# Moving the full loads of a softmax cross entropy from SyncE's ring to GpSimd's software ring

## Chip, cores, metric

The kernel runs on one core of one Trainium2 chip. The metric is the device time of one execution in microseconds (us), the median of the runs; a profiled execution gives the traces. The "span" of a profile is the profiled time of the core's instructions; it is about 2 us shorter than the metric.

Words used here: a *ring* is the queue in which the transfers of one issuing engine (SyncE, GpSimd) wait for the 16 DMA engines; a *descriptor* is one contiguous piece of a transfer; a *packet* is what the profile lists as one record of a DMA engine. A *gather* is a small transfer that fetches 128 single logits from addresses held in a tile. The *flag* is `single_packet=True` on a load.

## The reference

```python
def reference(logits, labels):            # logits [16, 512, 32000] float32, labels [16, 512]
    logits_max = np.max(logits, axis=-1, keepdims=True)
    log_sum_exp = np.log(np.sum(np.exp(logits - logits_max), axis=-1)) + logits_max.squeeze(-1)
    log_probs = logits - log_sum_exp[..., np.newaxis]
    loss = -log_probs[np.arange(batch)[:, None], np.arange(seq), labels]
    return loss.astype(np.float32)
```

1048.6 MB of logits must be read once. The kernel sums exponentials without subtracting the maximum, and fetches the 8192 logits at the labels by gathers.

## The kernel before

The 8192 rows are 128 partitions x 64 groups of 32000 logits. Three buffers of 128 x 16000 float32 (64000 B in each partition) take the loads in turn. Loads are numbered in order: 0, 1, 2 (4000, 4000 and 8000 columns) fill the first buffer, 3 to 126 fill one buffer each, and the last dozen, 127 to 138, are shorter, so that little work is left when the last byte lands.

```python
    plan(0, [[4000, 4000, 8000], [16000]], [(0, 0), (0, 1), (0, 2), (1, 0)])
    for g in range(1, G - 2):
        plan(g, [[W], [W]], [(0, 0), (1, 0)])
    ...                                                    # cut: the short last loads
    data = ctx.enter_context(tc.tile_pool(name="data", bufs=3))
    ...                                                    # cut: small tiles
    nc.scalar.dma_start(out=labs64[:], in_=labels_pg)
    nc.gpsimd.iota(idx[:], pattern=[[V, G]], base=0, channel_multiplier=G * V)
    nc.gpsimd.tensor_tensor(out=idx[:], in0=idx[:], in1=labs32, op=ALU.add)
    for g in range(G):                                     # 64 gathers of 128 single logits
        nc.gpsimd.indirect_dma_start(out=lab_logit[:, g:g + 1], out_offset=None, in_=lg,
            in_offset=bass.IndirectOffsetOnAxis(ap=idx[:, g:g + 1], axis=1))
    ...
    for j, (g, b, at, n) in enumerate(loads):
        ...                                                # cut: a new tile t for each buffer number b
        nc.sync.dma_start(out=t[:, at:at + n], in_=lg_pg[:, g, c0:c0 + n])
        exp(g, t[:, at:at + n])                            # ScalarE, in place, with a row sum
```

A load into a buffer waits until the exponential three buffers back has run.

The softmax here doesn't subtract the row's maximum and nothing guards it: scores larger than these inputs give would overflow.

## Time and profile before

| | before |
|---|---|
| time | 2435.71 us (2435.50 to 2435.98, 3 runs; the result below has a fourth) |
| rate over the span | 431 GB/s |
| ScalarE busy | 72% |
| one full load, mid-run (start of exponential to start of exponential) | 18.90 us, 8.192 MB: 433.5 GB/s |
| its exponential with the accumulator read | 13.64 us, then 5.27 us idle |

From the profile page of the kernel before: busy time of the engines, busy tenths of the DMA engines in 40 slices, and the packets, MB and share of 16 engines of its two main rings (q1 is SyncE's, q0 GpSimd's software ring).

```profile
...
DVE 1.3 (0%) x5; ACT 1748.9 (72%) x281; POOL 61.0 (3%) x70
...
DMA  9999999999999999999999999999999999999998
...
q1 hardware_dynamic: 20304, 1048.62, 99.8%
q0 software_dynamic: 2048, 0.04, 0.1%
...
```

The DMA engines are over 90% busy in every slice but the last, which has 80%: this kernel is bound by the loads. The 20304 packets of SyncE's ring are one for each partition row of each load (8 on each of 16 engines), one semaphore packet per engine and load (4 bytes that report the landing), and the outputs.

From the timeline of ScalarE before (start and duration in us; in brackets the idle time before it and what ended it), at the start, mid-run and at the end:

```profile
...
8.32 3.54 ACT L105 ACTIVATE t<-t 128x4000 f32<-128x4000 f32 x1 [5.86 <-DMA t<-in_logits_dram]
...
13.00 3.54 ACT L105 ACTIVATE t<-t 128x4000 f32<-128x4000 f32 x1 [1.05 <-DMA t<-in_logits_dram]
...
23.02 6.87 ACT L105 ACTIVATE t<-t 128x8000 f32<-128x8000 f32 x1 [6.39 <-DMA t<-in_logits_dram]
...
42.12 13.54 ACT L105 ACTIVATE t<-t 128x16000 f32<-128x16000 f32 x1 [12.13 <-DMA t<-in_logits_dram]
...
61.53 13.54 ACT L105 ACTIVATE t<-t 128x16000 f32<-128x16000 f32 x1 [5.79 <-DMA t<-in_logits_dram]
...
80.69 13.54 ACT L105 ACTIVATE t<-t 128x16000 f32<-128x16000 f32 x1 [5.52 <-DMA t<-in_logits_dram]
...
1597.17 13.54 ACT L105 ACTIVATE t<-t 128x16000 f32<-128x16000 f32 x1 [5.26 <-DMA t<-in_logits_dram]
...
1616.06 13.54 ACT L105 ACTIVATE t<-t 128x16000 f32<-128x16000 f32 x1 [5.27 <-DMA t<-in_logits_dram]
...
2372.73 13.54 ACT L105 ACTIVATE t<-t 128x16000 f32<-128x16000 f32 x1 [5.26 <-DMA t<-in_logits_dram]
...
2400.52 6.37 ACT L105 ACTIVATE t<-t 128x7400 f32<-128x7400 f32 x1 [0.46 <-DMA t<-in_logits_dram]
...
2430.02 1.00 ACT L105 ACTIVATE t<-t 128x960 f32<-128x960 f32 x1
...
```

The first six lines are the exponentials of loads 0 to 5, each run as soon as its load lands. Mid-run, starts lie 18.89 us apart with 5.26 us of idle time: ScalarE always waits for a DMA. The first of the ten short last loads make ScalarE wait 0.3 to 0.5 us each, the later ones 0.1 us or less, and the last exponential starts at 2430.02.

From the windows of the kernel before (the stretch in us, busy time of three engines, the granted clock, the DMA share, GB/s):

```profile
...
40.00:130.00 90.00, 0.00 (x0) 65.30 (x9) 19.72 (x21) 1.00 1.00 423
78.50:84.50 6.00, 0.00 (x0) 3.81 (x1) 1.88 (x2) 1.00 0.99 416
...
```

These stretches are shown for the comparison further down. 423 GB/s is less than 433.5 as gathers run here.

### The profile page before, as it was taken

The numbers are of one execution on the slowest core, as the hardware profiler recorded it, in microseconds if no ns is written. First come the engines' busy times: TensorE is split into PE (matmuls) and PEld (weight loads), VectorE is DVE, ScalarE is ACT, GpSimd is POOL, SyncE is SP. The second block draws the span as 40 slices with busy tenths as digits, with TensorE's granted clock in tenths as the row PEclk, the third lists the DMA queues.
The fourth block names the chain that finished last, engine by engine and source line by source line (L and its number), as shares of the span: only waits on it lengthen the run. The fifth ranks groups of instructions, "written<-read, shape, count | busy, mean of one in ns | idle before, by whom it ended". The sixth has DMA issues, their size and how long they took to land.

```text
span 2434.1 us, 807 instructions
## 1 busy us (share of the span) xinstructions
DVE 1.3 (0%) x5; ACT 1748.9 (72%) x281; POOL 61.0 (3%) x70
## 2 busy tenths in 40 slices
DVE  0000000000000000000000000000000000000000
ACT  4777766777677776777677776777667776777769
POOL 3222000000000000000000000000000000000000
DMA  9999999999999999999999999999999999999998
GB/s 421 422 421 433 425 438 431 427 438 438 433 426 436 438 434 426 435 438 434 426 435 436 435 430 431 436 435 430 431 436 438 431 427 436 438 433 426 438 433 377
DMA packets 22502, 1048.77 MB, mean 431 GB/s; under 512 B 4576, under 2 KB 4704, under 8 KB 5216
## 3 DMA queue, kind: packets, MB, share of 16 engines
q1 hardware_dynamic: 20304, 1048.62, 99.8%
q0 software_dynamic: 2048, 0.04, 0.1%
q10 hardware_dynamic: 144, 0.07, 0.0%
q14 instruction: 6, 0.05, 0.0%
HBM read 1048.67 MB, written 0.03 MB: 431 GB/s over the span
## 4 chain that ended last, share of the span: by engine, by line
DMA 76%; ACT 24%; issue 0%; SPq 0%; ACTq 0%; DVE 0%
DMA t<-in_logits_dram 76%; ACT t L105 24%; SPq L113 0%; ACTq L105 0%; ACT logsum_last L127 0%; DVE res_last L128 0%; ACT logsum L120 0%
## 5 line engine op out<-in xcount | busy, mean ns | idle before, releaser
L105 ACT ACTIVATE t<-t 128x16000 f32<-128x16000 f32 (+5 forms) x139 | 1734.8, 12481 | 681.4 <-DMA t<-in_logits_dram 681.2
L89 POOL DMA_INDIRECT lab_logit<-in_logits_dram,idx x64 | 60.3, 942 | 178.3 <-DMA lab_logit<-in_logits_dram,idx 174.5
L105 ACT ACTIVATION_READ_ACCUMULATOR t<-t 128x1 f32 x139 | 25.9, 186 | 0.0
L84 ACT ACT_TABLE_LOAD x1 | 1.3, 1283 | 1.2 <-PEq L144 1.2
L118 DVE TENSOR_REDUCE totals<-sums 128x63 f32<-128x315 f32 x1 | 0.5, 480 | 2398.9 <-ACT t L105 2398.9
L87 POOL TENSOR_TENSOR idx<-idx,labs 128x64 int32<-128x64 int32 x1 | 0.3, 322 | 7.5 <-DMA labs<-in_labels_dram 7.5
L85 DVE MEMSET sums<- 128x315 f32 x1 | 0.3, 321 | 0.9 <-PEq L144 0.9
L127 ACT ACTIVATE logsum_last<-sums_last,part 128x1 f32<-128x1 f32 x1 | 0.3, 294 | 0.0
L121 DVE TENSOR_TENSOR res<-logsum,lab_logit 128x63 f32<-128x63 f32 x1 | 0.2, 225 | 25.3 <-ACT logsum L120 25.3
L120 ACT ACTIVATE logsum<-totals 128x63 f32<-128x63 f32 x1 | 0.2, 238 | 0.0
L86 POOL IOTA idx<- 128x64 int32 x1 | 0.2, 172 | 0.4 <-PEq L155 0.4
L123 DVE TENSOR_REDUCE part<-sums_last 128x1 f32<-128x9 f32 x1 | 0.2, 163 | 4.0 <-ACT t L105 4.0
L128 DVE TENSOR_TENSOR res_last<-logsum_last,lab_logit 128x1 f32<-128x1 f32 x1 | 0.2, 159 | 1.2 <-ACT logsum_last L127 1.2
L144 POOL MEMSET const-uint8-127<- 128x1 uint8 x1 | 0.1, 118 | 0.0
L144 POOL MEMSET const-bfloat16-1.0<- 128x1 bf16 x1 | 0.1, 113 | 0.0
L144 POOL MEMSET const-float32-0.0<- 128x1 f32 x1 | 0.1, 98 | 0.2 <-issue 0.2
L144 POOL MEMSET const-float32-1.0<- 128x1 f32 x1 | 0.1, 104 | 0.0
## 6 DMA issues: line engine op xcount, KB each, us to landing
t<-in_logits_dram SPq DMA_DIRECT2D x124, 8000.0 KB, 43.0
t<-in_logits_dram SPq DMA_DIRECT2D x1, 5000.0 KB, 35.9
t<-in_logits_dram SPq DMA_DIRECT2D x2, 2000.0 KB, 9.6
t<-in_logits_dram SPq DMA_DIRECT2D x1, 4000.0 KB, 21.4
t<-in_logits_dram SPq DMA_DIRECT2D x1, 3700.0 KB, 32.9
t<-in_logits_dram SPq DMA_DIRECT2D x1, 3000.0 KB, 42.6
t<-in_logits_dram SPq DMA_DIRECT2D x1, 2920.0 KB, 39.5
t<-in_logits_dram SPq DMA_DIRECT2D x1, 2270.0 KB, 26.4
```

The costliest lines, as they stand in the source:

```text
L84: nc.scalar.preload_act_table_set("natural_log_exp_and_others")
L85: nc.vector.memset(sums[:], 0.0)
L86: nc.gpsimd.iota(idx[:], pattern=[[V, G]], base=0, channel_multiplier=G * V)
L87: nc.gpsimd.tensor_tensor(out=idx[:], in0=idx[:], in1=labs32, op=ALU.add)
L89: nc.gpsimd.indirect_dma_start(out=lab_logit[:, g:g + 1], out_offset=None, in_=lg, in_offset=bass.IndirectOffsetOnAxis(ap=idx[:, g:g + 1], ...
L105: nc.scalar.activation(out=ap, in_=ap, func=EXP, accum_out=s)
L118: nc.vector.reduce_sum(out=totals[:], in_=sums[:], axis=X)
L120: nc.scalar.activation(out=logsum[:], in_=totals[:], func=LN)
L121: nc.vector.tensor_tensor(out=res[:], in0=logsum[:], in1=lab_logit[:, 0:G - 1], op=ALU.subtract)
L123: nc.vector.reduce_sum(out=part[:], in_=sums_last[:, 0:K - 1], axis=X)
L127: nc.scalar.activation(out=logsum_last[:], in_=sums_last[:, K - 1:K], func=LN, bias=part[:])
L144: nc = _bacc.Bacc("TRN2", target_bir_lowering=False, num_devices=1)
```

## The change

The intent: let GpSimd issue the full loads on its software ring as one packet for each DMA engine, in place of one packet for each row, with one gather behind each of the first 64; keep the first four and the last loads, most of them short, on SyncE.

```diff
+    shared = range(4, 124)
+
+    def ring(j):
+        return nc.gpsimd if j in shared else nc.sync
...
-    for g in range(G):
+    def gather(g):
         nc.gpsimd.indirect_dma_start(
...
+    def load(j):
...
-        nc.sync.dma_start(out=t[:, at:at + n], in_=lg_pg[:, g, c0:c0 + n])
-        exp(g, t[:, at:at + n])
+        ring(j).dma_start(
+            out=buffers[b][:, at:at + n], in_=lg_pg[:, g, c0:c0 + n], single_packet=ring(j) is nc.gpsimd
+        )
+        if ring(j) is nc.gpsimd:
+            if to_gather:
+                gather(to_gather.pop(0))
+
+    loaded = 0
+    for j, (g, b, at, n) in enumerate(loads):
+        while loaded < len(loads) and loads[loaded][1] < b + 3:
+            load(loaded)
+            loaded += 1
+        exp(g, buffers[b][:, at:at + n])
```

## The prediction

> **What bounds it now.** DMA. The page gives the DMA engines 9 tenths in every slice, 431 GB/s over 2434 us; ScalarE is 72% busy, and the chain of waits is 76% loads. In the undisturbed middle (timeline of ScalarE) exponentials start every 18.90 us: one 8.19 MB load, 433.5 GB/s. An exponential takes 13.64 us, then ScalarE idles 5.27 us. The Trainium skill ("DMA: Bandwidth & Descriptors", Where 436 GB/s comes from) puts the ceiling at 435.2 GB/s; this trace is 0.4% under it, so little is left to win.
>
> **What can be won.** Packet records of the SyncE ring: one packet per partition row, 64000 B in 2361 ns, 40000 B in 1479, 252 B in 18: 0.03675 ns per byte plus 8.5 to 9 ns per packet. A load is 8 packets and a semaphore packet per engine. A gather's packet holds 8 descriptors and takes 15 ns, so descriptors inside a packet cost under 1 ns. One packet per engine should save 7 x 8.5 = 60 ns a load: 18.90 -> 18.84 us, over 120 loads -7 us. The 64 gathers now slow the first 14 full loads (19.0 to 19.4 us apart) by 4.7 us in all, 73 ns each against 24 ns for their own packets. Behind a load on its ring they may cost less: -1 to -3 us. Issue cost (about 1 us on GpSimd for a gather, 0.33 us on SyncE for a load) is hidden: a load is issued with 24 us of loads ahead of it.
>
> **What is lost at the start.** The skill's page (Queues, rings and completion order) says that an engine alternates between its rings packet by packet. The trace agrees: while both rings are full, gathers (two packets each) run every 4.8 us, two SyncE packets. After the change a software packet is 512000 B, 18.8 us, against 64000 B on SyncE, so a software load overtakes nearly all SyncE loads queued before it. Load 4 needs no free buffer; GpSimd reaches it at 9 us (after the labels), its data starts at about 13 us, where the first gather's does now. Load 2 then lands near 42 us instead of 23; its exponential frees buffer 0 at 49, load 5 is issued at 50 and overtakes load 3, which lands near 80 instead of 42. Only then can the exponential of buffer 1 run, though buffers 2 and 0 are full. Until it frees its buffer (93.5 us) no load can be issued: all engines idle from 79 to about 96 us (0.7 us landing, 13.64 us exponential, 2.5 us issue and start). That is +16 us, never regained.
>
> At the end SyncE's load 124 delays load 123 by two packets (4.7 us), within ScalarE's 5.27 us idle: no loss.
>
> **Sum:** 2435.7 + 16 - 7 - 2 = 2443 us; 80% range 2426 to 2453. Faster by over 2%: 0.01; within 2%: 0.94; slower: 0.05.
>
> **What would show it.** Timeline of ScalarE: exponential of load 2 at about 42 us, of load 3 at about 80, then three back to back; windows: DMA idle between 79 and 96. Mid-run period 18.82 to 18.85. Software packets of 512000 B, 18.8 us.
>
> **What would make it wrong.** If rings alternate by descriptor, load 3 is delayed less and the gap is 7 us or nothing: about 2427 to 2435. If packets don't overlap on the software ring (a bubble at every load or gather), the period grows; 0.4 us a load would bring +48 us, slower by 2%. If the record's per-packet cost isn't real engine time, the 7 us do not come: 2450.

## The result

| | before | after |
|---|---|---|
| time | 2435.61 us (2435.34 to 2435.98, 4 runs) | 2445.64 us (2445.45 to 2445.79, 4 runs) |
| span of the profile | 2434.1 us | 2443.7 us |
| ratio | | 1.0041, 95% interval 1.0024 to 1.0058 |

A ratio is the mean time of one kernel's runs over that of the other's of the same rounds, so it is not quite the ratio of the medians. The change costs 10 us, 0.4%.

From the profile page after, the same lines:

```profile
...
DVE 1.4 (0%) x5; ACT 1747.5 (72%) x281; POOL 129.4 (5%) x190
...
DMA  9999999999999999999999999999999999999998
...
q0 software_dynamic: 19328, 983.08, 93.2%
q1 hardware_dynamic: 3024, 65.57, 6.3%
...
```

The loads have moved to q0, but the packets have not been joined: 19328 is 120 loads x 16 engines x 8 rows (15360), their 1920 semaphore packets, and 2048 packets of gathers. The profile still lists one packet for each row.

From the timeline after; ScalarE's exponentials of loads 2 to 6 and GpSimd's issues of loads 4 to 6, then two exponentials mid-run, then those of loads 121 to 124 and the last one:

```profile
...
9.11 0.70 POOL L119 DMA_DIRECT2D t<-in_logits_dram  x1 [0.25 <-issue]
...
41.39 6.87 ACT L111 ACTIVATE t<-t 128x8000 f32<-128x8000 f32 x1 [24.76 <-DMA t<-in_logits_dram]
...
48.64 0.55 POOL L119 DMA_DIRECT2D t<-in_logits_dram  x1 [37.51 <-ACT t L111]
...
69.80 13.54 ACT L111 ACTIVATE t<-t 128x16000 f32<-128x16000 f32 x1 [21.46 <-DMA t<-in_logits_dram]
...
83.34 13.52 ACT L111 ACTIVATE t<-t 128x16000 f32<-128x16000 f32 x1
83.73 0.56 POOL L119 DMA_DIRECT2D t<-in_logits_dram  x1 [33.24 <-ACT t L111]
...
96.86 13.52 ACT L111 ACTIVATE t<-t 128x16000 f32<-128x16000 f32 x1
...
110.38 13.52 ACT L111 ACTIVATE t<-t 128x16000 f32<-128x16000 f32 x1
...
1604.07 13.54 ACT L111 ACTIVATE t<-t 128x16000 f32<-128x16000 f32 x1 [5.27 <-DMA t<-in_logits_dram]
...
1622.97 13.54 ACT L111 ACTIVATE t<-t 128x16000 f32<-128x16000 f32 x1 [5.27 <-DMA t<-in_logits_dram]
...
2285.12 13.54 ACT L111 ACTIVATE t<-t 128x16000 f32<-128x16000 f32 x1 [5.27 <-DMA t<-in_logits_dram]
...
2306.36 13.54 ACT L111 ACTIVATE t<-t 128x16000 f32<-128x16000 f32 x1 [7.61 <-DMA t<-in_logits_dram]
...
2344.16 13.54 ACT L111 ACTIVATE t<-t 128x16000 f32<-128x16000 f32 x1 [24.17 <-DMA t<-in_logits_dram]
...
2357.70 13.52 ACT L111 ACTIVATE t<-t 128x16000 f32<-128x16000 f32 x1
...
2439.63 0.98 ACT L111 ACTIVATE t<-t 128x960 f32<-128x960 f32 x1
...
```

From the windows after, the stretches shown of before:

```profile
...
40.00:130.00 90.00, 0.00 (x0) 66.38 (x11) 7.74 (x10) 1.00 0.93 398
78.50:84.50 6.00, 0.00 (x0) 6.00 (x3) 0.56 (x1) 1.00 0.00 0
...
```

Read against the lines of before. **Start:** the exponential of load 2 starts at 41.39 us, not 23.02, and that of load 3 at 69.80, not 42.12. Load 3's has to end before its buffer is free; only then, at 83.73, can load 6 be issued. By then all loads issued so far have landed, and the windows show engines that do nothing from 78.5 to 84.5. Over 40 to 130 us the core moves 398 GB/s where the kernel before, with more gathers, moved 423. **Middle:** starts lie 18.90 us apart, as before. The hoped-for gain of packets is not there. **End:** load 123's exponential waits until 2344.16, 37.80 us after the one before it. By the time it has run, load 124 is there, and the later loads land before ScalarE gets to them; from here on ScalarE, no longer DMA, sets the pace, and the last exponential starts at 2439.63 without a wait.

Why loads 2, 3 and 123 come late is seen in the packets of the two rings. From the DMA view after, restricted to 51 to 66 us, when loads 3 and 5 are under way (packets, MB, share of 16 engines):

```profile
...
q1 hardware_dynamic: 48, 3.07, 47.3%
q0 software_dynamic: 48, 3.07, 47.3%
...
```

The same view of the same run from 2303 to 2337 us, when loads 123 and 124 are under way:

```profile
...
q1 hardware_dynamic: 115, 7.36, 50.0%
q0 software_dynamic: 114, 7.17, 48.7%
...
```

48 and 48, 115 and 114 packets, nearly all of 64000 B. Equal counts over so long a stretch could also come from larger units taken in turn, but the packet records show equal counts at the finest step too: in each 4.73 us from 2303.65 to 2336.76, the time of two packets, the 16 engines start 16 packets of each ring. The engines take one packet from each ring in turn, so two such loads that share the engines each take twice as long. From 14 to 38 us load 4 (64000 B a packet) shares with load 2 (32000 B) in the same way: the view lists 96 packets and 6.14 MB on the software ring, 112 packets and 3.58 MB on SyncE's. Eight packets of load 4 alternate with eight of load 2, so nearly all of load 4 goes through before load 2 ends, 18.4 us late.

So the theory (A): **the software ring moves data exactly as fast, and the loss is lost order.** Where a ring takes over, a later load on the new ring shares the engines with an earlier one on the old ring, which ScalarE needs first; the buffers come free late, and either the engines run dry (start) or ScalarE is left with a backlog that it cannot work off any more (end). The rival (B): the software ring costs something of its own (descriptor writing, first start, a fixed price of changing rings), or the one-packet flag does. A small model of theory A, two rings that alternate by descriptor, gave the expectation of `sw_4_126`, which names it.

### The profile page after: what moved, and what is told of

The parts are those of the page before. It is cut to its first block, busy times and chain, and to the rows that moved or that the text cites. A ratio compares the mean times of both kernels' runs of the same rounds, so it can differ in the third digit from the quotient of the medians.

```text
span 2443.7 us, 801 instructions
## 1 busy us (share of the span) xinstructions
DVE 1.4 (0%) x5; ACT 1747.5 (72%) x281; POOL 129.4 (5%) x190
## 3 DMA queue, kind: packets, MB, share of 16 engines
q0 software_dynamic: 19328, 983.08, 93.2%
## 4 chain that ended last, share of the span: by engine, by line
issue 44%; DMA 38%; ACT 15%; another core or an unknown queue 2%; POOL 1%; POOLq 0%; SPq 0%; ACTq 0%; DVE 0%
DMA t<-in_logits_dram 38%; ACT t L111 15%; POOL t L119 1%; POOL lab_logit L94 0%; POOLq L119 0%; SPq L119 0%; ACTq L111 0%; ACT logsum_last L145 0%; DVE res_last L146 0%; ACT logsum L138 0%
## 5 line engine op out<-in xcount | busy, mean ns | idle before, releaser
L119 POOL DMA_DIRECT2D t<-in_logits_dram x120 | 64.9, 541 | 2121.0 <-ACT t L111 2120.8
```

What stands on the lines that cost most here:

```text
L119: ring(j).dma_start(out=buffers[b][:, at:at + n], in_=lg_pg[:, g, c0:c0 + n], single_packet=ring(j) is nc.gpsimd)
```

## The experiments

Eleven kernels, each with 3 rounds beside the kernel before on its chip (medians of before there: 2435.79, 2435.78 and 2435.76 us). All gave correct results but one.

| kernel | time, us | against before |
|---|---|---|
| change without the flag | 2445.67 | +9.88 |
| GpSimd has loads 6 to 123 | 2438.23 | +2.44 |
| 4 to 121 | 2443.08 | +7.29 |
| 4 to 125 | 2455.66 | +19.87 |
| 6 to 138 (to the end) | 2436.14 | +0.36 |
| 6 to 99 | 2435.43 | -0.33 |
| all | 2436.86 | +1.10 |
| change, GpSimd's descriptors 16000 B, flag on | 2464.19 | +28.41 |
| the same, flag off | 2464.24 | +28.46 |
| before, descriptors 16000 B | 2445.90 | +10.12 |
| before without gathers (wrong result) | 2430.91 | -4.85 |

### 1. The flag off

```diff
-            ... single_packet=ring(j) is nc.gpsimd
+            ... single_packet=False
```

> The change with the one-packet flag off, nothing else. Theory A (the flag leaves no mark on 64000-byte descriptors: engines alternate between rings descriptor by descriptor, and each descriptor pays its 9 ns, flag or not): within 0.5 us of the change (2445.6), load 3's exponential again at 69.8 us, period 18.97 us with a gather and 18.90 without. Theory B (the flag does make a unit of a load, which costs or saves time): load 4 no longer holds load 2 back by its whole 18.4 us, so the early exponentials start at other times, or the period moves by 0.05 us or more (6 us in all).

Measured 2445.67 us; the change has 2445.64. From the profile page of this kernel:

```profile
...
q0 software_dynamic: 19328, 983.08, 93.2%
...
```

The same 19328 packets as with the flag, and load 3's exponential at 69.72 us. The flag left no mark on time, packets or order. Theory B falls as far as the flag goes, and with it every gain and every loss that the prediction drew from one packet for each engine.

### 2. The start: GpSimd begins at load 6

```diff
-    shared = range(4, 124)
+    shared = range(6, 124)
```

> GpSimd's loads begin at load 6 instead of 4, so loads 0 to 5, all that start without a free buffer or early, stay in order on SyncE. Theory A (the 9.6 us are 6.6 us of idle engines at the start because ring alternation put loads 2 and 3 behind 4 and 5, and about 3 us of backlog at the end): start loss gone, engines busy at 78 to 86 us, time 7 us under the change, about 2438.5. Theory B (the start loss is the software ring's own first start, its descriptor writing and landing): a gap of several us appears around the first GpSimd load again, time near 2445.

Measured 2438.23 us, 7.4 under the change. The windows of this kernel:

```profile
...
40.00:130.00 90.00, 0.00 (x0) 59.12 (x9) 6.39 (x8) 1.00 1.00 432
78.50:84.50 6.00, 0.00 (x0) 0.00 (x0) 0.00 (x0) 1.00 0.84 363
...
```

432 GB/s from 40 to 130 us in place of 398: (432 - 398) / 432 x 90 us = 7.1 us, nearly all of the gain. GpSimd's first load again overtakes: load 6 shares with the end of load 4 and with load 5, and the exponential of load 5 starts only at 98.13 us. But load 5 is now the only late one, other loads are queued meanwhile, and the engines never run dry. ScalarE idles through the short window above and it costs nothing. Theory B wanted a new gap at the first GpSimd load: there is none.

### 3. The end: hand-back two loads earlier, and two later

```diff
-    shared = range(4, 124)
+    shared = range(4, 122)      # sw_4_122
+    shared = range(4, 126)      # sw_4_126
```

> SyncE takes the loads back two loads earlier (122). Theory A (at the hand-over SyncE's load shares the engines one to one with the software load before it, which then lands 18.9 us late; ScalarE is left with a backlog of about 18 us that it works off at 5.3 us a load): two more full loads let it work off its backlog, so about 3 us under the change, 2442.6. Theory B (the end costs a fixed price for changing rings, wherever it falls): same as the change, 2445.6.

> SyncE takes the loads back two loads later (126). Theory A: less full loads left to work off the backlog in, so ScalarE ends later: a small model of two rings that alternate by descriptor says 9 us over the change, about 2454.5. Theory B (fixed price of changing rings): same as the change, 2445.6.

Measured 2443.08 (expected 2442.6) and 2455.66 us (expected about 2454.5). From the timeline of the first, the exponentials of loads 121 and 125:

```profile
...
2306.74 13.54 ACT L111 ACTIVATE t<-t 128x16000 f32<-128x16000 f32 x1 [24.17 <-DMA t<-in_logits_dram]
...
2361.08 13.54 ACT L111 ACTIVATE t<-t 128x16000 f32<-128x16000 f32 x1 [0.15 <-DMA t<-in_logits_dram]
...
```

From that of the second, the exponential of load 125:

```profile
...
2380.93 13.54 ACT L111 ACTIVATE t<-t 128x16000 f32<-128x16000 f32 x1 [23.28 <-DMA t<-in_logits_dram]
...
```

In the first, load 121's exponential is as late (24.17 us of idle time before it), but from 2361 us on ScalarE waits for its loads again: the backlog is worked off. In the second, ScalarE runs without a wait from 2380.93 us to the end. A fixed price of changing rings would have given 2445.6 twice. The delay is about the same each time; what it costs depends on how much idle time ScalarE has left after it.

### 4. No hand-back

```diff
-    shared = range(4, 124)
+    shared = range(6, 139)      # sw_6_139
+    shared = range(6, 100)      # sw_6_100: hand-back in mid-run
```

> GpSimd's loads from 6 to the very end, so no hand-over back to SyncE. Theory A (all of the loss is order lost at the two hand-overs; the software ring itself moves data just as fast, and a gather costs 73 ns wherever it stands): no backlog at the end, time that of the kernel before within 1 us, 2435.6. Theory B (the software ring costs something by itself, most for the ten short last loads at 0.55 us of GpSimd each): 2438 or more, that is no better than beginning at load 6 and ending at 124.

> GpSimd has loads 6 to 99, SyncE the rest: both hand-overs lie where ScalarE has time to work off its backlog. Theory A: the hand-back at 100 costs one idle stretch of the engines of about 0.5 us (as at 2358 us in the change) and no backlog at the end: 2436.6, that is 1.6 us under sw_6_124 (2438.2). Theory B (a hand-back costs its 2 to 3 us wherever it falls): 2438.2.

Measured 2436.14 us for the first: 2.1 under sw_6_124, so that is what the hand-back at 124 costs, and 0.36 over before, inside the interval of the ratio (0.9985 to 1.0018). The ten short last loads cost nothing that shows on GpSimd's ring. The second took 2435.43 us, 1.2 below the expectation. Its engines do idle at the hand-back, about 0.3 us at 1897 us in the packet records, and load 99's exponential comes 37.79 us after the one before it, as load 123's does in the change; nothing of it is left at the end. Theory B's 2438.2 is out. That it is 0.7 us faster than `sw_6_139` theory A does not say. The traces show where: the last exponentials start at 2429.82 and 2429.76 us, so the loads are equally fast, and 0.5 us arise after the last output is issued (2.33 against 2.83 us to the end of the span). Why stays open.

### 5. Everything on GpSimd

```diff
-    shared = range(4, 124)
+    shared = range(0, 139)
...
+            if j == 4:
+                index()                       # iota and add, moved behind the first five loads
-            if to_gather:
+            if j >= 4 and to_gather:
```

> All loads on GpSimd, the index work moved behind the first five so that the first load does not wait for the labels; no hand-over at all. Theory A: no idle stretch after the start and no backlog at the end; the first load's data start about 1 to 1.7 us later than on SyncE (GpSimd's first gather took about 3 us from issue to data beside other loads, SyncE's first load 1 us), so 2437 to 2437.8. Theory B (the software ring costs something of its own at each load): more than 2439.

Measured 2436.86 us, just under the range. The first exponential starts at 9.00 us instead of 8.32. GpSimd issues its first load only at 1.30 us, SyncE in the kernel before at 0.74 (timelines; GpSimd's times are rough), and the first packets start at 2.67 and 1.75 us, that is 1.37 and 1.01 us after these issues. So 0.56 us are GpSimd's later issue, and 0.36 us a later first byte, once; a small part of the two is not seen at the first exponential. Mid-run, loads lie 18.90 us apart as before, and the last exponential starts at 2430.41, only 0.39 us later than before: no cost for each load shows. The rest of the loss lies after the last output is issued (3.04 us to the end of the span, 2.45 before). The Trainium skill ("DMA: Bandwidth & Descriptors", Specifications) has about 1 us to the first byte for GpSimd and 0.6 for SyncE; the difference of 0.4 agrees with the 0.36 us seen here, while both times are longer here when counted from the issue.

### 6. Descriptors of 16000 B

GpSimd's loads in the change are cut into 16000-byte descriptors, 32 on each engine where the change has 8, with the flag and without; and the loads of the kernel before are cut likewise on SyncE.

```diff
-            ... single_packet=ring(j) is nc.gpsimd
+            ... single_packet=ring(j) is nc.gpsimd, **({"max_dma_last_dim": 16000} if ring(j) is nc.gpsimd else {})
```

> The change with GpSimd's loads cut into 16000-byte descriptors (32 per engine and load, where the change has 8), flag on. Theory C (the flag does nothing: each descriptor is a packet of its own and pays about 9 ns): period 18.90 + 24 x 0.009 = 19.12 us, +26 us over 120 loads; at the start 16000 bytes go against SyncE's 32000, so load 2 lands near 28 us and load 3 near 51, the start gap of 6.6 us goes: 2445.6 + 26 - 7 = 2465. Theory D (the flag does merge descriptors, only those of 64000 bytes are too long for it): period 18.84 to 18.90, and if the merged packet is the unit of alternation, load 4 overtakes load 2 and load 5 load 3 as the prediction had it, with 16 us of idle engines at about 80 us: about 2448.

> The same cut to 16000 bytes, flag off. Theory C: as d16_flag within 1 us, about 2465. Theory D: period near 19.12 us and no start gap, about 2465, that is clearly apart from d16_flag.

> The kernel before with all loads cut to 16000-byte descriptors on SyncE. Packets there cost 8.5 to 9 ns each by their records (16000 bytes in 596 ns); if that is engine time, the period is 19.12 us and the time 2435.7 + 27 = 2463. If the 9 ns of the records overlap with the next packet, the period stays 18.90 and the time 2436: then the 7 us that the prediction counted on could never have come.

Measured 2464.19 and 2464.24 us: again no difference by the flag, with descriptors of a quarter of the size. From the profile page of the first (packets, MB, share):

```profile
...
q0 software_dynamic: 65408, 983.08, 93.2%
...
```

From its timeline, the exponentials of loads 2, 3 and 123:

```profile
...
27.14 6.87 ACT L111 ACTIVATE t<-t 128x8000 f32<-128x8000 f32 x1 [10.59 <-DMA t<-in_logits_dram]
...
51.38 13.54 ACT L111 ACTIVATE t<-t 128x16000 f32<-128x16000 f32 x1 [17.28 <-DMA t<-in_logits_dram]
...
2362.67 13.54 ACT L111 ACTIVATE t<-t 128x16000 f32<-128x16000 f32 x1 [36.02 <-DMA t<-in_logits_dram]
...
```

From its windows, the stretch of the start and one near the end:

```profile
...
40.00:130.00 90.00, 0.00 (x0) 66.89 (x9) 7.09 (x8) 1.00 1.00 426
2361.00:2376.00 15.00, 0.00 (x0) 13.33 (x1) 0.00 (x0) 1.00 0.01 3
...
```

65408 packets are 120 x 16 x 32 and the same 3968 others: with the flag, one for each descriptor. Theory D is out. The shares follow the sizes, as theory C said: 16000 against 32000 bytes, load 2 lands near 27 us (28 expected), load 3 near 51 (51 expected), and the start gap is gone (426 GB/s from 40 to 130 us).

The time was expected at 2465 and measured at 2464, but **the sum was right by accident; two of its terms were wrong.** The period grew from 18.90 to 18.98 us, not to 19.12: 0.08 us for 24 more descriptors is about 3.3 ns each, not 9, and 120 loads bring some 9.6 us, not 26. The rest is at the end, where nothing was expected: SyncE's 64000-byte packets now take four times the share of GpSimd's 16000-byte ones, load 123's exponential starts only at 2362.67 us, and the engines stand still from 2361 to 2376 us. It is the start of the change in a mirror. From the change: -7 (start gap, run 2), +9.6 (period), and about +16 (idle at the end, 16.5 us in the packet records, where the change has 0.5) make 2445.6 + 18.6 = 2464.2.

On SyncE the cut cost 10.1 us where 27 were expected: 128 x 0.078 = 10.0 us, 3.2 ns for each added descriptor. The 9 ns of the records are mostly not engine time. The page of this kernel says so itself:

```profile
...
q1 hardware_dynamic: 68944, 1048.62, 100.2%
...
```

The packets' own time sums to more than the span of 16 engines: the records overlap. They may not be added up.

### 7. No gathers

The kernel before, its gathers replaced by a memset (the result is wrong).

```diff
-    for g in range(G):
-        nc.gpsimd.indirect_dma_start(...)
+    nc.vector.memset(lab_logit[:], 0.0)
```

> The kernel before without its 64 gathers (label logits set to zero, so the result is wrong on purpose). If each gather costs the engines 73 ns, as the widened periods say: 2435.7 - 4.7 = 2431.0. If they only share in a time that something else sets: 2435.7. In the change the periods with a gather are 0.075 us wider too, so the same 4.7 us are in it, and no part of the 1 to 3 us that the prediction expected from placing them behind loads came.

Measured 2430.91 us: 64 gathers cost 4.85 us, 76 ns each. In the change the 60 or so loads with a gather behind them lie 18.97 us apart and the later ones 18.90, so a gather costs 70 to 75 ns there too: behind a load on its ring or between the packets of another ring, the price is the same. That the gather's two packets take only 24 ns by the records does not say what it costs.

## Why the prediction was right, and where it was not

The time (2443 predicted, 2445.6 measured) fell inside the range. By terms, its mechanism was right in kind, and its size right by luck.

| step of the prediction | predicted | the runs |
|---|---|---|
| loads bind; ring and rate leave next to nothing to win | | right: loads all on GpSimd +1.1 us, 18.90 us a load on both rings |
| idle engines at the start, as loads 4 and 5 overtake 2 and 3 | +16 | right in kind, +7.4 (change less sw_6_124) |
| hand-back at the end | 0 | +2.1 (sw_6_124 less sw_6_139) |
| one packet for each engine saves 60 ns a load | -7 | 0 (flag off: the same time) |
| gathers cheaper behind loads | -2 (-1 to -3) | 0 (70 to 76 ns each in both kernels) |
| sum | +7 | +9.9; the terms above and +0.4 of sw_6_139 over before |

The three differences in the last column follow one another (change, `sw_6_124`, `sw_6_139`, before), so their sum is right by construction; what supports them is that each was expected beforehand and that the traces show the idle time and the waits.

- **"a software packet is 512000 B, 18.8 us, against 64000 B on SyncE"** was the failing step. The profile lists 8 packets on each engine for a load, flag or not (runs 1 and 6), and the rings alternate by these. Load 2 did land when predicted (41.4 us), since eight packets of load 4 alternate with its eight; load 5, predicted to overtake load 3 whole, came when half of load 3 was done and alternated with the other half. So load 3 landed at 69.8 us, not 80, and the gap was less than half. The prediction had named this case ("If rings alternate by descriptor") and put the gap at 7 us or nothing; its total for that case, 2427 to 2435, was wrong, as it kept the packet gain that falls with the same assumption. The other case that it named, that the cost in the records is not real engine time (2450), came true as well; it had not put the two together.
- **"One packet per engine should save 7 x 8.5 = 60 ns a load"** had two faults: no packets were joined, and the 8.5 ns of a record are not engine time. By run 6 a descriptor costs 3.2 to 3.3 ns, so even joined packets could have saved at most about 7 x 3.2 = 22 ns a load, 2.7 us in all (an estimate from that run).
- **"SyncE's load 124 delays load 123 by two packets (4.7 us), within ScalarE's 5.27 us idle: no loss"** followed from the same wrong packet size. The two share one to one for some 35 us. Load 123's exponential starts at 2344.16 us, where 2285.12 (load 121's) + 2 x 18.90 = 2322.92 was due: 21 us late, with 15 exponentials left, most of them short, in which to work off the backlog. Run 3 shows the price change by -2.6 and +10 us as the hand-back moves by two loads.
- **"Behind a load on its ring they may cost less"**: they do not (run 7).

The wrong gains (-9) and the oversized loss (+16 for 7.4 and 2.1) cancelled to within 3 us. Not settled: whether the software ring did write one packet and the engines switch inside it, or whether the flag had no effect at all. The profile shows the same packets either way. It can list several pieces as one: a gather's data appear as one 32-byte packet on each engine, 8 logits from 8 addresses. But no load is listed so, with the flag or without, and the time and the order do not show it either. No version beat the kernel before clearly: the best, sw_6_100, has a ratio of 0.9999 (0.9982 to 1.0015). What is left to win in it is small: all gathers together are 4.85 us, 0.2%.

## What to carry to other kernels

A second ring added no bandwidth, as the loads already filled the engines (18.90 us a load on both); what it changed was the order in which loads landed. Where two rings held loads at once, the engines took their descriptors in turn (64000 B against 64000, 32000 or 16000), so each load got a share by its descriptor size, and a consumer that takes loads in order gets the older one late: hand over only where the consumer has idle time left to recover, as at load 100 here, and not within the first or last few buffers. And when a sum of predicted terms matches the measured time, test the terms one by one: here, twice, a right sum hid wrong parts.

## What the Trainium skill lacked or had wrong

- "DMA: Bandwidth & Descriptors", Queues, rings and completion order: it says that an engine drains a whole packet, typically 9 to 17 descriptors, from one ring before it switches. The loads' rings switched after each 64000-byte row (48 against 48 packets in 15 us, 16 against 16 in each 4.73 us), or each 16000-byte piece when cut so, with the one-packet flag on and off. It lacks what this means for order: two loads on two rings share the engines in proportion to descriptor size (load 2 lands at 41.4 us beside 64000-byte descriptors, 27.1 us beside 16000-byte ones, 23.0 us with all loads on one ring).
- The same page, SWDGE vs HWDGE vs iDMA, gives 4096 B as preferable for a packet and at most 64 descriptors. It does not say that 8 descriptors of 64000 B or 32 of 16000 B are not joined in effect: 19328 and 65408 listed packets, times equal within 0.1 us.
- The same page, Why small descriptors are slow: it gives a fixed cost of about 3 cycles for each packet inside the engine, and that section does not say how profile records show it. Here an added 16000-byte descriptor costs about 3.3 ns on GpSimd's ring and 3.2 on SyncE's, while its record carries 8.5 to 9 ns over its bytes' time; "Perfetto Trace Analysis", DMA Engine Tracks, says that the slices show actual busy time; here the packets' times sum to 100.2% of 16 engines' span in one run, so they overlap and are no cost to add up.
- The same page, Rules for kernel authors, that spreading loads over issuing engines does not help bandwidth: agrees (18.90 us a load on both rings). It lacks that it can cost time by order: 10 us here, 20 us with the hand-back two loads later.
- No page has the cost of a small gather to a full stream of loads: 76 ns for each gather of 128 single elements, three times the 24 ns of its own packets.
